# A hybrid decoder step on one core: the inversion's transfers issued side by side from three queues, and weight splits allowed during a norm's sums

## The chip, the cores and the metric

One Trainium2 chip; the kernel runs on one of its cores. The metric is the device time of one execution in microseconds, the median of several runs.

## The reference

One step of a decoder layer over two groups of rows: a prompt of 256 rows and 8 samples of 8 rows, so 320 columns in all when the activations are held transposed (d_model 2048 as 16 chunks of 128 partitions by 320 columns). All tensors are fp32.

```python
mod = silu(c) @ w_ada + b_ada                     # 2048 -> 6*2048
h = rmsnorm(x, g_pre_mix) * (1 + sc1) + sh1
proj = h @ w_in                                   # 2048 -> 5136: q, k, v, z, a, b, u
# group A: conv and silu on q, k, v; 8 heads of 128, chunked gated delta rule
lmat = strict_lower(kb @ k.T * decay)             # per chunk and head
tinv = inverse(I + lmat)                          # triangular solve
u, w = tinv @ (v * beta), tinv @ (kb * exp(gcum))
# group B: S5 state space, gelu, GLU with w_glu, rmsnorm
mix = concat([o, y5]) @ w_out
x = x + gt1 * rmsnorm(mix, g_post_mix)
h = rmsnorm(x, g_pre_ffn) * (1 + sc2) + sh2
f = (silu(h @ w_gate) * (h @ w_up)) @ w_down      # d_ff 5632
x = x + gt2 * rmsnorm(f, g_post_ffn)
```

## The kernel before

**Weights.** Every weight matrix goes through TensorE in blocks of 128 x 1024 numbers (512 KB), each a `Seg`, in one written-out list. A block is loaded by SP (`load`, line 467) into one of 12 buffers. For w_in, w_glu, w_out, w_gate, w_up and w_down it is then split (`do_split`, line 496): ScalarE writes the rounded part `whi`, VectorE the rest `wlo`, and TensorE makes three fast products for each 128 x 128 tile (`mm3`, line 504), with the activations split in the same way. w_ada's blocks aren't split. They are used as they are, four at a time, against 9 columns; the sums of 512 columns are evacuated to a buffer of the same 12 (`adaev`) and transposed (`ada_tail`, line 766).

**Order.** The kernel's order is written out by a planner at build time. It keeps a clock for each engine and for the transfers, and walks the list of blocks. Between any two products of a block it calls `tick`, which advances the background work: generators, each of which yields until the operation that it has next would start soon by these clocks (`fits`, line 168). So each engine gets a fixed order, and the chip's semaphores do the rest. The order of the list around the change: w_in's last slab, w_glu (16 blocks, with 2048 columns of w_ada), w_out's first half (the S5 group's rows; 16 blocks, with 1024 columns of w_ada), w_out's second half (the eight heads' rows, 16 blocks), 1024 columns of w_ada (10240 to 11263), and then the FFN.

**The inversion.** In the background of w_glu and of w_out's first half runs the delta rule of the prompt and that of the samples. `invert` (line 1727) inverts two unit triangular matrices of 128 x 128 for each of the 8 heads. The 16 x 16 diagonal blocks of all of them are turned, through DRAM, into one tile with one block on each partition: 6 writes (the blocks to `inv0`, zeros to `inv1` and `inv2`), 8 small reads into Y, then a substitution in 15 steps on VectorE, 16 small write-backs (from Y and X), 4 reads into Wc and Tc. Products of 32 x 32 and 64 x 64 tiles on TensorE put the blocks together. `chunks` (8 heads, three at a time) then needs the result; `samples` needs none of it and runs beside it. When both are done the heads are ready for w_out's second half.

In the planner a transfer is due to start when its operands are free. What counts for a transfer's output is also the last write to it, by whatever engine, and a DRAM tensor counts as one piece:

```python
for r in (rd.get(k), la.get(k)):
    if r and r[1] != eng:
        t = max(t, r[0] + 0.2)
```

so a transfer that writes `inv1` waits until the one before it is due to have landed.

**The norm ahead of the FFN.** `residual` (line 2373) sums squares over all chunks with products against ones, makes the row factors, and starts `modulate2` (line 2408) for the 16 chunks, four at a time, which writes the FFN's split input h2. From the sums on until four chunks of h2 are written out, `quiet` is set, and `pump` (line 443) splits no further block. `pump` otherwise splits up to 4 blocks ahead (`AHEAD`) of those loaded. `fetch` (line 437) loads the next block whenever more than 3 (`WRES`) of the 12 buffers are free.

Of the kernel before, what the change touches and what calls it, by code (L numbers as in the profile page):

```python
# [23 lines left out]
N = NP + NS  # L24
# [86 lines left out]
class Layer:  # L111
# [36 lines left out]
            e += x * (n - 1)  # L148
        return [(nm, i) for i in range(f // g, e // g + 1)]

    def _start(self, eng, outs, ins, same):

        t = 0.0
        rd, la = self.rd, self.la
        for ap in ins:
            for k in self._keys(ap):
                r = rd.get(k)
                if r:
                    t = max(t, r[0] + (same if r[1] == eng else 0.2))
        for ap in outs:  # L160
            for k in self._keys(ap):
                for r in (rd.get(k), la.get(k)):
                    if r and r[1] != eng:
                        t = max(t, r[0] + 0.2)
                t = max(t, self.war.get(k[0], 0.0) + 0.2)
        return t

    def fits(self, eng, outs, ins):

        c = self.clk  # L170
        t = self._start(eng, outs, ins, 0.0)
        if eng == "PE":
            return t <= c["now"] + self.EPS_PE
        return (eng == "SP" or c[eng] <= c["now"] + self.LIM) and t <= max(c[eng], c["now"]) + self.EPS
# [268 lines left out]
    def pump(self, force=-1):  # L443

        self.fetch()
        while self.ns < min(self.cur + self.AHEAD, self.nl):
            s = self.segs[self.ns]
            if self.ns > force and (self.quiet or s.t > self.clk["now"] or s.split and len(self.wfree) < 3):
                break
            if s.split:  # L450
                self.do_split(s)
                self.wput(s.raw)
            self.ns += 1

    AHEAD, WRES = 4, 3

    def ws(self, name, dt=F32):

        i = self.wfree.pop(0)
        t = self._slot(self.wp.tile([128, 1024], dt, name=name, tag="ws%d" % i, bufs=1), "ws%d" % i, 1)  # L460
        self.wslot[t.name] = i
        return t
# [217 lines left out]
    def xw(self, name="xw"):  # L680
        return self._slot(self.mp.tile([128, 356], F32, name=name, tag="xw", bufs=self.CAP["xw"]), "xw", self.CAP["xw"])

    def dma(self, out, in_, eng=None):
        n = 1
        for d in out.shape:
            n *= d
        q = "SP" if eng in (None, self.nc.sync) else "ACT" if eng is self.nc.scalar else "POOL"
        if self.dry:
            self.sig = q, (out,), (in_,)
            return  # L690
        self.stage_end = max(self.stage_end, self._dma(q, n, out, in_))
        return (eng or self.nc.sync).dma_start(out, in_)
# [1034 lines left out]
    def invert(self):  # L1727

        nc, V, G = self.nc, self.V, self.G
        L = self.L  # L1730
        q_ = nc.sync
        yield from self.take("xw", 7)
        yield from self.take("t4")
        v = lambda t: t[:, :256].rearrange("p (h q) -> p h q", h=8)
# [1 line left out]
        dL, dT, dW = (self.dp.tile([4, 32, 16, 32], F32, name="inv%d" % i) for i in range(3))  # L1736
        Tc = [self.xw("Tc") for _ in range(2)]
        Wc = [self.xw("Wc") for _ in range(2)]
# [7 lines left out]
        yield  # L1746
        flat = lambda d: d.rearrange("b r (c h) q -> c (b r) (h q)", c=2)
        for c in range(2):
            yield from self.p.dma(flat(dL)[c], Tc[c][:, :256], q_)
            for d in (dT, dW):  # L1750
                yield from self.p.dma(flat(d)[c], Wc[0][:, :256], q_)
        G.memset(X[:, 0:256:17], 1.0)
        G.memset(T, 0.0)
        yield
# [1 line left out]
        Yv = Y[:, :256].rearrange("p (r q) -> p r q", r=16)  # L1756
        blk = lambda d, s, b: d[b, 16 * s:16 * s + 16, :, 16 * s:16 * s + 16].rearrange("r h q -> h r q")
        for s in range(2):
            for b in range(4):
                p0 = 64 * s + 16 * b  # L1760
                yield from self.p.dma(Yv[p0:p0 + 16], blk(dL, s, b), q_)
        yield
        yield from self.p.ts(Y[:, :256], Y[:, :256], -1.0, OP.mult)
        for i in range(1, 16):
# [10 lines left out]
        for t, d in ((Yv, dW), (Xv, dT)):  # L1775
            for s in range(2):
                for b in range(4):
                    p0 = 64 * s + 16 * b
                    yield from self.p.dma(blk(d, s, b), t[p0:p0 + 16], q_)
        yield  # L1780
        for t, d in ((Wc, dW), (Tc, dT)):
            for c in range(2):
                yield from self.p.dma(t[c][:, :256], flat(d)[c], q_)
        yield
        Pt = [X, Y]

# [621 lines left out]
    def modulate2(self, kt, rm, rs):  # L2408
        x = self.M[kt]
        yield from self.p.mul(x, x, rm)  # L2410
        yield from self.p.add(x, x, self.xr[kt][:, :N], eng=self.V if kt < self.QUIET else self.G)
        a, sh = self.A[:, kt, :], self.mod[:, 48 + kt, :]
        t = self.xw("h2t")
        yield from self.p.stt(t[:, :NP], x[:, :NP], a[:, 0:1], rs[:, :NP], OP.mult, OP.mult)
        v = t[:, NP:N].rearrange("p (b i) -> p b i", i=8)
        e = self.G
        yield from self.p.mul(t[:, NP:N], x[:, NP:N], rs[:, NP:N], eng=e)
        yield from self.p.mul(v, v, a[:, 1:9, None].to_broadcast([128, 8, 8]), eng=e)
        yield from self.p.add(v, v, sh[:, 1:9, None].to_broadcast([128, 8, 8]), eng=e)
        yield  # L2420
        hl = self.p3.tile([128, 2, N], F32R, name="h2", bufs=16)
        yield from self.p.act(hl[:, 0, :NP], t[:, :NP], AF.Identity, bias=sh[:, 0:1])
        yield from self.p.copy(hl[:, 0, NP:], t[:, NP:N])
        yield
        yield from self.p.stt(hl[:, 1, :NP], t[:, :NP], sh[:, 0:1], hl[:, 0, :NP].bitcast(F32), OP.add, OP.subtract)
        yield from self.p.sub(hl[:, 1, NP:], t[:, NP:N], hl[:, 0, NP:].bitcast(F32))
        self.h2[kt] = hl
# [4 lines left out]
    def ffn(self):  # L2432
        I = self.I

        def start():
            self.bp_close()
            self.p3 = self.p12.enter_context(self.tc.tile_pool(name="p3", bufs=1))
            self.await_(lambda: self.mod_ready.issuperset(range(48, 80)))
            self.set_A(0, 16, 64, "g_pre_ffn")
            self.await_(lambda: "xr" in self.flags)  # L2440
            self.bg(self.residual(), front=True)

        self.fn(start)
        self.items += self.ada_set(self.ADA[4], self.ADA[5])
        self.fT = {}
# [6 lines left out]
        def fbuf():  # L2452
            self.fbase = self.mp.tile([128, 13, 2, N], F32R, name="f", tag="xcat")

        def gu(s, w, f, bank=None):
            self.await_(lambda: hasattr(self, "h2") and all(k in self.h2 for k in range(s.k0, s.k0 + s.nk)))
            if f == 0 and s.k0 == 0 and w == "g":
                fbuf()
            for m in range(s.ncol // 128):
                key = (w, f + m)  # L2460
                if s.k0 == 0:
                    self.gps[key] = self.mbank(bank[m] if bank else self.rot())
                ps = self.gps[key]
                self.mm3(s, ps[:, :N], m, act_h, s.k0 == 0, s.k0 + s.nk == KT)
                if s.k0 + s.nk == KT:
                    ps = self.gps.pop(key)
                    if w == "g":
                        t = self.gs = self.xw("gs")
                        self.act(t[:, :N], ps[:, :N], AF.Silu)
                        self.gsd[f + m] = t  # L2470
                    else:
                        self.bg(self.f_tail(f + m, ps), front=True)
# [3 lines left out]
        for k0 in range(0, KT, 4):  # L2476
            segs.append(Seg(wg, k0, 4, 0, 256, lambda s: gu(s, "g", 0, ("bA", "bA"))))
            segs.append(Seg(wu, k0, 4, 0, 256, lambda s: gu(s, "u", 0, ("bB", "bB"))))
            if k0 % 8:
                segs.append(Seg(wg, k0 - 4, 8, 256, 128, lambda s: gu(s, "g", 2, ("mm",))))  # L2480
                segs.append(Seg(wu, k0 - 4, 8, 256, 128, lambda s: gu(s, "u", 2, ("mm",))))
# [173 lines left out]
```

## Time and profile before

| | us |
|---|---|
| median of 3 runs | 1825.05 |
| lowest, highest | 1821.77, 1828.55 |
| the profiled execution | 1823.18 |
| its span, first to last instruction | 1821.4 |
| mean granted TensorE clock in it | 0.977 of full speed |

The span is what the profile's rows divide up. The granted clock is 1 at 2.4 GHz and 0.5 at 1.2 GHz.

### The profile page before, as it was taken

The page shows a single profiled execution, that of the slowest core. Times are in us where ns is not written, and L with a number is a line of the kernel's source. Part 1 is how long each engine was busy: PE and PEld are TensorE (multiplying, and loading weights), DVE is VectorE, ACT ScalarE, POOL GpSimd, SP SyncE. Part 2 cuts the span into 40 slices and gives each one's busy share as a digit, 9 for nine tenths or more (in the row PEclk, how much of TensorE's full clock was granted, in tenths as well). Part 3 has the DMA queues.
Part 4 walks back from the last instruction along what each step waited for, and adds up shares of the span by engine and source line. Part 5 has one row for each costly group of instructions (what it writes and reads, how often), then busy time and mean ns, then how long its engine had stood idle before and what let it go on. Part 6 is the DMA issues. An engine that isn't in the chain of part 4 may idle for free.

```text
span 1821.4 us, 32727 instructions
## 1 busy us (share of the span) xinstructions
PE 1731.8 (95%) x12961; PEld 1600.4 (88%) x12961; DVE 987.7 (54%) x1840; ACT 768.9 (42%) x1439; POOL 335.0 (18%) x439
## 2 busy tenths in 40 slices
PE   7899998898999889997999999999999999999997
PEld 4678997776787769995999999999999999999997
DVE  3587842788865556677633434444443444444455
ACT  3433334677744434664433333333333333333343
POOL 1000185556132212065300000000000000000043
PEclk8999998999999989998999999999999999999998
DMA  8898744776858956758465565554565545655452
GB/s 275 297 369 287 193 111 129 230 217 209 262 172 257 301 172 179 225 165 289 128 185 174 150 183 169 149 150 122 153 176 151 151 119 152 180 150 149 117 154 80
DMA packets 501262, 340.66 MB, mean 187 GB/s; under 512 B 45355, under 2 KB 452619, under 8 KB 500781
## 3 DMA queue, kind: packets, MB, share of 16 engines
q1 hardware_dynamic: 483904, 332.41, 59.5%
q10 hardware_dynamic: 16838, 5.93, 1.3%
q8 instruction: 102, 1.67, 0.4%
q14 instruction: 50, 0.41, 0.1%
q0 software_dynamic: 368, 0.24, 0.1%
HBM read 323.22 MB, written 14.54 MB: 185 GB/s over the span
## 4 chain that ended last, share of the span: by engine, by line
PE 67%; DVE 3%; ACT 1%; issue 1%; DMA 1%; ACTq 0%; SPq 0%; DVEq 0%
PE ps_mm L319 34%; PE ps_bA L319 17%; PE ps_bB L319 14%; PE ps_ax L319 2%; DVE acc L281 1%; DVE wlo L502 1%; PE ps_bA L333 1%; ACT hT L264 0%; DVE u L281 0%; PE ps_mm L333 0%; DVE P L281 0%; DMA inv<-Y 0%; DMA raw<-in_w_ada_dram 0%; ACT whi L501 0%; DMA S<-in_state_delta_dram 0%
## 5 line engine op out<-in xcount | busy, mean ns | idle before, releaser
L502 DVE TENSOR_TENSOR wlo<-raw,whi 128x1024 fp32r<-128x1024 f32 (+2 forms) x441 | 502.6, 1142 | 554.3 <-ACT whi L501 327.2
L501 ACT ACTIVATE whi<-raw 128x1024 fp32r<-128x1024 f32 (+2 forms) x441 | 424.4, 965 | 412.3 <-DVE wlo L502 309.4
L319 PE MATMUL ps_mm<-h,whi 128*128 128x320 f32 x1376 | 303.4, 308 | 0.0
L319 PE MATMUL ps_mm<-hT,whi 128*128 128x320 f32 x1204 | 290.6, 328 | 2.9 <-ACT hT L264 1.5
L319 PEld LDWEIGHTS ps_mm<-h,whi 128*128 128x128 f32 x1376 | 229.9, 187 | 0.8 <-issue 0.8
L319 PEld LDWEIGHTS ps_mm<-hT,whi 128*128 128x128 f32 x1204 | 202.8, 193 | 14.9 <-issue 6.2
L319 PE MATMUL ps_mm<-h,wlo 128*128 128x320 f32 x688 | 211.6, 307 | 0.0
L319 PE MATMUL ps_mm<-hT,wlo 128*128 128x320 f32 x602 | 189.2, 314 | 2.2 <-DVE wlo L502 2.2
L319 PE MATMUL ps_bA<-h,whi 128*128 128x320 f32 x736 | 166.3, 313 | 3.2 <-DVE h L281 3.0
L319 PE MATMUL ps_bB<-h,whi 128*128 128x320 f32 x704 | 156.0, 309 | 0.0
L319 PE MATMUL ps_mm<-f,whi 128*128 128x320 f32 x704 | 155.5, 308 | 0.0
L281 POOL TENSOR_TENSOR sqa<-acc 128x320 f32<-128x320 f32 x1 | 0.7, 722 | 841.1 <-DVE acc L281 841.1
L319 PEld LDWEIGHTS ps_bA<-h,whi 128*128 128x128 f32 x736 | 125.9, 192 | 4.5 <-DVE h L281 3.3
L319 PEld LDWEIGHTS ps_mm<-h,wlo 128*128 128x128 f32 x688 | 128.9, 187 | 0.0
L319 PEld LDWEIGHTS ps_bB<-h,whi 128*128 128x128 f32 x704 | 118.4, 189 | 0.8 <-issue 0.8
L319 PEld LDWEIGHTS ps_mm<-hT,wlo 128*128 128x128 f32 x602 | 115.5, 192 | 3.5 <-DVE wlo L502 3.5
L319 PEld LDWEIGHTS ps_mm<-f,whi 128*128 128x128 f32 x704 | 117.3, 187 | 0.8 <-ACT whi L501 0.8
L319 PE MATMUL ps_bA<-h,wlo 128*128 128x320 f32 x368 | 115.1, 313 | 1.7 <-DVE wlo L502 1.7
L319 PE MATMUL ps_mm<-f,wlo 128*128 128x320 f32 x352 | 108.5, 308 | 0.4 <-DVE wlo L502 0.4
L319 PE MATMUL ps_bB<-h,wlo 128*128 128x320 f32 x352 | 108.6, 308 | 0.0
L319 PE MATMUL ps_ax<-raw,cs 128*32 128x512 f32 (+2 forms) x832 | 99.6, 588 | 6.9 <-DMA raw<-in_w_ada_dram 6.9
L319 PE MATMUL ps_mm<-hx,whi 128*128 128x320 f32 x328 | 81.1, 333 | 3.3 <-ACT whi L501 3.3
(594 smaller groups left out, 2900.7 us busy)
## 6 DMA issues: line engine op xcount, KB each, us to landing
raw<-in_w_ada_dram SPq DMA_DIRECT2D x180, 512.0 KB
raw<-in_w_gate_dram SPq DMA_DIRECT2D x88, 512.0 KB
raw<-in_w_up_dram SPq DMA_DIRECT2D x88, 512.0 KB
raw<-in_w_in_dram SPq DMA_DIRECT2D x66, 512.0 KB
raw<-in_w_down_dram SPq DMA_DIRECT2D x64, 512.0 KB
raw<-in_w_out_dram SPq DMA_DIRECT2D x32, 512.0 KB
raw<-in_w_down_dram SPq DMA_DIRECT2D x64, 192.0 KB
raw<-in_w_glu_dram SPq DMA_DIRECT2D x16, 512.0 KB
```

The source lines that it names most:

```text
L281: return e.tensor_tensor(out, a, b, op=op)
L319: return self.T.matmul(out, lhsT, rhs, start=start, stop=stop)
L333: return self.T.transpose(out, in_, self.ident[b:b + p, b:b + p])
L501: return (self.S.activation(s.hi[:, :w], s.raw[:, :w], AF.Copy), self.V.tensor_tensor(s.lo[:, :w], s.raw[:, :w], s.hi[:, :w].bitcast(F32), ...
L502: self.V.tensor_tensor(s.lo[:, :w], s.raw[:, :w], s.hi[:, :w].bitcast(F32), op=OP.subtract))
```

## The change

The planner gets a flag `beside`: a transfer that has it no longer counts the transfers that last wrote its output. All transfers of `invert` get it. The 6 writes and the 16 write-backs move from SP's queue to ScalarE's, the 4 last reads to POOL's; the 8 reads into Y stay on SP. While the FFN's start is under way (`deep`, from the start of `residual` to the first product with w_gate), `pump` may go on during `quiet` and beyond 4 blocks, until two blocks that need a split lie ahead. In `modulate2` the residual add of chunks 2 and 3 moves from VectorE to POOL.

```diff
-    def _start(self, eng, outs, ins, same):
+    def _start(self, eng, outs, ins, same, dma=False):
...
-                    if r and r[1] != eng:
+                    if r and r[1] != eng and not (dma and r[1] == "DMA" and r is rd.get(k)):
                         t = max(t, r[0] + 0.2)
...
     def fits(self, eng, outs, ins):
 
         c = self.clk
-        t = self._start(eng, outs, ins, 0.0)
+        dma = eng[-1] == "*"
+        eng = eng.rstrip("*")
+        t = self._start(eng, outs, ins, 0.0, dma)
...
     def pump(self, force=-1):
 
         self.fetch()
-        while self.ns < min(self.cur + self.AHEAD, self.nl):
+        while self.ns < self.nl:
             s = self.segs[self.ns]
-            if self.ns > force and (self.quiet or s.t > self.clk["now"] or s.split and len(self.wfree) < 3):
+            if sum(x.split for x in self.segs[self.cur:self.ns]) > 1 if self.deep else self.ns >= self.cur + self.AHEAD:
+                break
+            if self.ns > force and (self.quiet and not self.deep or s.t > self.clk["now"] or s.split and len(self.wfree) < 3):
                 break
...
-    def dma(self, out, in_, eng=None):
+    def dma(self, out, in_, eng=None, beside=False):
...
-            self.sig = q, (out,), (in_,)
+            self.sig = q + "*" * beside, (out,), (in_,)
...
-        q_ = nc.sync
+        q_, qs, ql = nc.sync, nc.scalar, nc.gpsimd
...
         for c in range(2):
-            yield from self.p.dma(flat(dL)[c], Tc[c][:, :256], q_)
+            yield from self.p.dma(flat(dL)[c], Tc[c][:, :256], qs, beside=True)
             for d in (dT, dW):
-                yield from self.p.dma(flat(d)[c], Wc[0][:, :256], q_)
+                yield from self.p.dma(flat(d)[c], Wc[0][:, :256], qs, beside=True)
...
-                yield from self.p.dma(Yv[p0:p0 + 16], blk(dL, s, b), q_)
+                yield from self.p.dma(Yv[p0:p0 + 16], blk(dL, s, b), q_, beside=True)
...
-                    yield from self.p.dma(blk(d, s, b), t[p0:p0 + 16], q_)
+                    yield from self.p.dma(blk(d, s, b), t[p0:p0 + 16], qs, beside=True)
         yield
         for t, d in ((Wc, dW), (Tc, dT)):
             for c in range(2):
-                yield from self.p.dma(t[c][:, :256], flat(d)[c], q_)
+                yield from self.p.dma(t[c][:, :256], flat(d)[c], ql, beside=True)
...
-        yield from self.p.add(x, x, self.xr[kt][:, :N], eng=self.V if kt < self.QUIET else self.G)
+        yield from self.p.add(x, x, self.xr[kt][:, :N], eng=self.V if kt < 2 else self.G)
...
             self.bg(self.residual(), front=True)
+            self.deep = True
...
             if f == 0 and s.k0 == 0 and w == "g":
+                self.deep = False
                 fbuf()
```

## Rows read from the trace of the kernel before

**Rows 1.** The page: TensorE and the others, busy time, share of the span, instructions.

```profile
PE 1731.8 (95%) x12961; PEld 1600.4 (88%) x12961; DVE 987.7 (54%) x1840; ACT 768.9 (42%) x1439; POOL 335.0 (18%) x439
```

**Rows 2.** Busy time by stretch: length, PE, PEld, DVE, ACT, POOL; clock, DMA share, GB/s.

```profile
555.00:648.00 93.00, 86.47 (x627) 69.27 (x625) 52.68 (x131) 42.60 (x76) 24.88 (x42) 1.00 0.91 288
648.00:683.00 35.00, 26.62 (x742) 22.92 (x742) 17.58 (x41) 10.04 (x21) 3.45 (x8) 0.85 0.50 159
683.00:769.00 86.00, 85.47 (x658) 77.60 (x656) 56.81 (x147) 51.09 (x150) 10.66 (x20) 1.00 0.64 191
769.00:827.00 58.00, 57.38 (x391) 56.49 (x393) 45.79 (x62) 32.56 (x58) 37.05 (x41) 1.00 0.65 200
827.00:876.00 49.00, 35.74 (x208) 26.28 (x205) 37.46 (x71) 19.51 (x40) 28.35 (x52) 0.79 0.67 234
876.00:1821.40 945.40, 935.32 (x6381) 927.87 (x6379) 407.43 (x479) 338.64 (x443) 47.06 (x63) 0.99 0.52 151
```

**Rows 3.** Timeline of SP's queue: start, duration of the issue, transfer, count.

```profile
556.14 0.34 SPq L692 DMA_DIRECT2D inv<-Tc  x1
...
559.51 0.33 SPq L692 DMA_DIRECT2D Y<-inv  x1
...
579.19 1.86 SPq L692 DMA_DIRECT2D Y<-inv  x1
...
601.10 0.33 SPq L692 DMA_DIRECT2D inv<-Y  x1
...
642.93 1.15 SPq L692 DMA_DIRECT2D Wc<-inv  x2
```

**Rows 4.** Timeline of PE: start, duration, product, count, [idle before it <- releaser].

```profile
648.21 1.29 PE L319 MATMUL ps_bA<-Wc,L 32*32 32x32 f32 x128
...
659.91 0.21 PE L319 MATMUL ps_bB<-Tc,X 32*32 32x32 f32 x1 [3.32 <-issue]
...
666.20 0.21 PE L319 MATMUL ps_bB<-Tc,Y 32*32 32x32 f32 x1 [4.69 <-issue]
...
769.14 0.45 PE L319 MATMUL ps_mm<-hz,whi 128*128 128x320 f32 x2
```

**Rows 5.** The tile inv: its write-backs on SP, shortest/median/longest issue in ns.

```profile
L692 SPq DMA_DIRECT2D inv<-Y x8: 327/644/1988, 601.1 to 626.8; - x8
L692 SPq DMA_DIRECT2D inv<-X x8: 423/559/1892, 627.7 to 642.1; - x8
```

**Rows 6.** Transfers of POOL's queue: KB each, us from issue to landing.

```profile
vr<-in_b_ada_dram POOLq DMA_DIRECT2D x1, 48.0 KB, 5.4
wr<-in_w_conv_dram POOLq DMA_DIRECT2D x1, 48.0 KB, 8.6
```

**Rows 7.** Timeline of ScalarE: one issue of a transfer, and one split.

```profile
70.30 0.44 ACTq L692 DMA_DIRECT2D craw<-in_c_re_dram  x1
...
592.09 1.06 ACT L501 ACTIVATE whi<-raw 128x1024 fp32r<-128x1024 f32 x1 [5.62 <-DVE P L281]
```

**Rows 8.** Timeline of PE where the FFN starts.

```profile
847.58 1.11 PE L333 MATMUL ps_mm<-ident,adaev 128*128 128x128 f32 x4 [8.37 <-ACT adaev L264]
...
850.93 0.63 PE L319 MATMUL ps_bA<-h,wlo 128*128 128x320 f32 x1 [1.71 <-DVE wlo L502]
...
867.03 0.63 PE L319 MATMUL ps_bA<-h,whi 128*128 128x320 f32 x1 [3.03 <-DVE h L281]
```

**Rows 9.** Timelines of VectorE, ScalarE and POOL in the norm ahead of the FFN.

```profile
835.18 0.49 DVE L281 TENSOR_TENSOR ms<-ps_bA,rs 128x320 f32<-128x320 f32 x1 [4.69 <-PE ps_bA L319]
...
838.05 0.49 DVE L281 TENSOR_TENSOR u<-u,xr 128x320 f32<-128x320 f32 x1
...
845.76 0.86 POOL L281 TENSOR_TENSOR u<-u,xr 128x320 f32<-128x320 f32 x1
...
846.00 1.04 ACT L501 ACTIVATE whi<-raw 128x1024 fp32r<-128x1024 f32 x1
...
849.65 1.23 DVE L502 TENSOR_TENSOR wlo<-raw,whi 128x1024 fp32r<-128x1024 f32 x1
```

More of the change, by code (lines that the diff above doesn't have):

```diff
@@ L455 @@
     AHEAD, WRES = 4, 3
+    deep = False
     def ws(self, name, dt=F32):
```

## The prediction

> **What bounds the kernel now.** I read the engines' busy times first: TensorE is busy 1731.8 us of the span [rows 1], so only TensorE's holes can be won. Then the busy time by stage [rows 2]: the reader subtracts TensorE's busy time from each stretch. From 876 us on it lacks 10.1 of 945.4 us, and nothing in the change reaches that part. From 683 to 827 us it lacks 1.1. What is left is 555 to 648 us (6.5 idle; the inversion's transfers run here), 648 to 683 us (8.4 idle and a granted clock of 0.85, 35 × 0.15 = 5.3 more; the inversion's matmuls) and 827 to 876 us (13.3 idle, clock 0.79; the norm ahead of the FFN). About 40 us is all that the change can touch. The timelines of SP, PE, ScalarE and VectorE in these stretches gave the rest.
>
> **Part 1, the chain of the inversion.** The order on SP [rows 3] shows it: first write 556.14, reads of Y from 559.51 to 579.19, write-backs from 601.10, last reads 642.93, while the first matmul on the result starts at 648.21 [rows 4]. 92 us, of which VectorE's substitution takes about 15 (the last read is issued by 581.05, lands within the 5.3 us below, near 586, and the write-backs begin at 601). The write-backs alone spread over 41.8 us, because the planner held each one until the one before it was due to have landed. The new flag takes that wait away. Worked out: the 8 reads cost SP about 0.53 each, 4.2 us, and land within the 5.3 us that the last reads took (642.93 to 648.21); Y is there near 569 and not near 586. The 16 write-backs go out in 16 × 0.6 (the medians of both kinds [rows 5]), 9.6 us, and land in 5.3: 15 in place of 41.8. The last 4 reads move to POOL's queue, where a transfer takes 5.4 to 8.6 us to land [rows 6], against 5.3. The chain ends 17 + 27 − 2, about 42 us earlier.
>
> What this buys: the chain has to end before w_out's second half, which needs the eight heads. That half starts at 769.14 [rows 4], and in the 86 us before it TensorE lacks 0.5 us [rows 2]. So TensorE does not wait for the heads. It takes their matmuls in between the blocks of w_out's first half; earlier heads only push these blocks back. What is late next is TensorE's own list. Value: 0. Bounds: 0, and the gaps that the chain itself makes. Of these there are two, 3.32 and 4.69 us within the 32x32 matmuls [rows 4], released by nothing the profile shows, with the clock's dip after them (0.85 over the stretch): 8.4 + 5.3 = 13.7 us. The same matmuls are issued afterwards, into a stretch with more transfers under way (DMA share 0.91 against 0.50), so I keep the gaps. The other small holes of 555 to 648 us, 6.5 us, may shrink: the inversion holds 7 of the 12 xw buffers and a sample needs 3, so earlier release lets two samples and the chunks overlap. I take −2, bounds 0 to −6.5.
>
> **Part 1, the cost on ScalarE.** 6 writes and 16 write-backs are now ScalarE instructions. One issue there took 0.44 us [rows 7]; on SP the write-backs took 0.33 to 1.99 [rows 5]. The 6 cost 6 × 0.44 = 2.6 us and fall beside ScalarE's idle time. The 16 come as one block (the planner books 0.1 us each, 1.6 together) and hold ScalarE for 9.6 us, 5.3 at the least and 16 if each took 1.0. Queued behind them are the `whi` halves of the next w_glu blocks, the tanh of the gates and the copy of `adaev`; TensorE waits for each of these in its own order. The cover is ScalarE's idle time in this stretch, for instance 5.62 us before 592.09 [rows 7]. If it is used up the cost is 9.6 − 5.6 = 4.0 us of TensorE; I take +4, bounds 0 and +9.6. Each issue also waits for its source (Tc, Wc's zeros, X, Y), but the planner asks for that before it emits, so the waits are short.
>
> **Part 1, POOL.** The 4 last reads wait on POOL for the 16 write-backs. Queued behind them are a sample's two masks and the squares of the GLU's rows, and TensorE waits for the masks. The result lands 0.1 to 3.3 us later than through SP, and now TensorE's first 32x32 matmul may stand at the head of its queue meanwhile, where today it starts without a wait. I take +1.5, bounds 0 and +3.3. SP loses 26 of its issues, but no wait of TensorE for a weight load is among the holes from 555 to 683 us, so that is worth 0.
>
> **Part 2, the two FFN blocks.** Today the first block of w_gate gets its `whi` at 846.00 and its `wlo` at 849.65, after the norm, and TensorE waits 1.71 us for it at 850.93, having waited 8.37 for the evacuation of the w_ada columns that stands behind that `whi` on ScalarE, and 3.03 for h2 later [rows 8, 9]. VectorE is idle for 4.69 us during the sums [rows 9], so there is room for a split. But the block is not there to be split. A block is loaded only when more than 3 of the 12 weight buffers are free. While `quiet` holds, the eight blocks of w_ada's columns 10752 to 11263 hold 8 of them, the evacuated sums of columns 10240 to 10751 hold 1 (`ada_tail` gives it back only after `quiet`, and until then the eight cannot be used up), and 3 are kept: 12. So `pump` stops at the last loaded block, whatever `deep` allows, and the first w_gate block is loaded and split where it is now, after `quiet`. Only the w_up block can come somewhat earlier, and TensorE does not wait for that one today. The two residual adds go from VectorE (0.49 each) to POOL (0.86) [rows 9]: VectorE gains 1.0 us, POOL's row of work for the first four h2 tiles grows by 1.7, with about 1 us of slack. Value of part 2: 0. Bounds: +2 (POOL late by 0.7 to 2) and −9 (below).
>
> **Sum.** The profiled execution took 1823.18 us, 1.8 around its span. 0 − 2 + 4 + 1.5 + 0 = +3.5 gives 1826.7. The runs' median is 1825.05, 1.9 above that execution, so I say 1828: the same within what a measurement of this kernel can tell (0.5%, 9 us).
>
> **Rivals.**
> A. *Faster: the inversion's gaps close.* If the 32x32 matmuls, at their new place, come with wide matmuls in between, both gaps and the dip go: 3.5 − 13.7 = −10.2, 1815. For it: the first 128 of them took 1.29 us without a gap [rows 4]. Against: the next 256 had two. It decides from about 9 us of the 13.7. The Trainium skill ("Runtime: NRT & Kernel Launch", Instruction fetch mechanics) says that refilling an engine's instruction memory is mostly hidden; if the gaps are such refills, the trace disagrees today, and by that rule they would go.
> B. *Slower: the block of issues stops TensorE.* If none of ScalarE's idle time covers it, TensorE loses 9.6 us where I booked 4 and then a spell at 1.2 GHz, as after the gaps at 659.91 and 666.20, 5.3 us: 3.5 + 5.6 + 5.3 = +14, 1839. For it: ScalarE's results are waited for in TensorE's order. Against: 5.62 us of idle time on ScalarE. It decides from an issue of 0.8 us on.
> C. *The FFN blocks are split during the sums after all.* Then the `whi` leaves the copy's way (1.04 us), the 1.71 goes and up to 3.03, and some of the dip (clock 0.79 over 49 us): −5.8 − 3, with part 1 as above: −5.3, 1820; alone it is worth −9. For it: the idle 4.69 us. Against: the count of buffers.
> D. *POOL's reads come late.* If each of the 4 reads waited its turn for a landing of 8.6 us in place of 5.3, the chain ends 13 us later than booked, and TensorE stands for a part of it, 4 us: 1832. The Trainium skill ("SBUF — State Buffer", SBUF: two separate sides) says that descriptors of POOL's transfers are written by GpSimd and are kept from it while VectorE runs some of its copies, and that ScalarE's or SP's queue avoids this; no run here shows it yet. By the rule the landing is longer than the rows' 8.6.
>
> **How the numbers follow.** The forecast (1820 to 1834) 0.48, A 0.13, B 0.18, C 0.11, D 0.10. Faster by over 0.5%, below 1815.9: most of A and half of C, 0.18. Slower, above 1834.2: most of B, a little of D and of the forecast, 0.23. The same: 0.59. The range goes from A's far side, 1813, to B, 1841.
>
> **What would show it.** Right: SP shows no write-back any more, ScalarE a block of 16 issues of some 0.6 us each; the first 32x32 matmul comes about 40 us earlier; w_out's second half starts within 6 us of 769; the first w_gate block still has its `wlo` after the first h2 tiles. Wrong: a `whi` of w_gate between the sums and 838 us (C); no "issue" gap among the 32x32 matmuls (A); a TensorE wait of over 5 us on ScalarE beside the block of issues, or on POOL's landing (B, D). The forecast also falls if the new order of the list moves TensorE's holes elsewhere, after 683 us, where there are none now.

## The result, and the profile after

| | before | after |
|---|---|---|
| median, us | 1826.38 (4 runs) | 1837.29 (4 runs) |
| lowest, highest | 1821.77, 1828.55 | 1836.00, 1840.38 |
| span of the profiled execution | 1821.4 | 1838.6 |

The ratio is 1.0075 (95% interval 1.0052 to 1.0098): slower, by 11 us in the medians. That is inside the range, outside the forecast's own 1820 to 1834, and within 2 us of rival B's 1839. The profile's first part of the kernel after, to be held against [rows 1], shows TensorE busy 6.7 us longer; the rest of the longer span is idle time.

```profile
PE 1738.5 (95%) x12961; PEld 1603.3 (87%) x12961; DVE 987.6 (54%) x1838; ACT 770.7 (42%) x1441; POOL 340.9 (19%) x445
```

**Cut at the same instructions.** The stage borders of [rows 2] fall on other work now, so I cut both traces at three TensorE instructions that bear the same work: the samples' first `sP,kb` product, the first `hz` product (w_out's second half), and the transposes of `adaev` ahead of the FFN (at 847.58 before). Ahead of the first mark TensorE's order did not change, yet its time varies from 554.6 to 563.8 us over the executions profiled here (e5 aside). Whoever compares spans takes this scatter along. The windows, of before and then of after; the first number behind each is its length:

```profile
558.40:769.14 210.74, 196.19 (x1993) 168.08 (x1993) 124.06 (x309) 102.15 (x242) 36.63 (x64) 0.98 0.74 230
769.14:847.58 78.44, 69.45 (x473) 61.62 (x471) 60.08 (x91) 41.02 (x76) 46.17 (x58) 0.96 0.76 248
847.58:1821.40 973.82, 958.86 (x6500) 948.89 (x6500) 430.46 (x519) 349.70 (x465) 66.28 (x98) 0.99 0.51 150
```

```profile
562.72:786.32 223.60, 203.33 (x1992) 172.38 (x1993) 122.77 (x308) 102.64 (x243) 37.92 (x68) 0.95 0.73 224
786.32:869.94 83.62, 69.93 (x473) 61.64 (x471) 64.78 (x95) 42.04 (x78) 48.84 (x64) 0.95 0.64 202
869.94:1838.60 968.66, 956.89 (x6500) 947.25 (x6500) 427.92 (x513) 349.85 (x465) 69.21 (x94) 0.99 0.52 151
```

The counts of matmuls agree to within one, so each stretch holds the same products. The first is 12.9 us longer: idle 20.3 against 14.6 us (+5.7), busy 203.3 against 196.2 (+7.1 for the same products; the clock, below, accounts for it). The second is 5.2 longer, the third 5.2 shorter. The sum is +12.9.

**The first stretch.** ScalarE's timeline after, where the write-backs now stand:

```profile
588.62 0.58 ACT L266 ACTIVATE adaev<-ps_ax 128x512 f32<-128x512 f32 x1
588.64 0.84 ACTq L697 DMA_DIRECT2D inv<-Y  x2
589.10 0.43 ACT L266 ACTIVATE gt<-ps_mm 128x320 f32<-128x320 f32 x1
589.58 5.44 ACTq L697 DMA_DIRECT2D inv<-Y  x6
595.05 5.79 ACTq L697 DMA_DIRECT2D inv<-X  x8
600.94 0.38 ACT L266 ACTIVATE sP<-ps_bA 128x256 f32<-128x256 f32 x1 [11.41 <-DMA raw<-in_w_ada_dram]
```

From 588.64 to 600.84, 12.2 us, ScalarE issues 16 transfers, and it computes nothing from 589.53 on. A row of the timeline joins issues that follow one another and holds the time between them too, so 0.76 us for each is the pace of the block and not the length of an issue. The issues themselves, shortest/median/longest in ns:

```profile
L697 ACTq DMA_DIRECT2D inv<-Y x8: 310/432/525, 588.6 to 594.6; - x8
L697 ACTq DMA_DIRECT2D inv<-X x8: 309/459/642, 595.1 to 600.4; - x8
```

Together they take 6.9 us, the 0.44 of [rows 7] for each. The other 5.3 us lie between them, and 4.7 of those in three waits: 2.66 us up to 593.70, 0.73 up to 597.93 and 1.29 up to 599.53. By the trace's record of semaphores (the counters by which instructions wait for one another) each of the three issues waits for the counter of an earlier write-back of the block, and starts 0.02 us after that one has landed. In this program the transfers of SP and ScalarE share eight such counters, and POOL's have eight of their own, so a long row of transfers has to wait for its own landings.

Behind the block stands `sP`, the evacuation that the next sample's products need. VectorE waits for it, and TensorE for VectorE (VectorE's timeline, then TensorE's; what the dots stand for is left out here and below):

```profile
601.36 0.60 DVE L301 TENSOR_SCALAR kr<-ps_bA,dk 64x128 f32<-64x128 f32 x2 [9.68 <-ACT sP L266]
...
602.11 1.19 PE L321 MATMUL ps_bA<-sP,kb 128*128 128x128 f32 x4 [7.99 <-DVE kr L301]
```

The releaser named for TensorE is VectorE's `kr`; that one had itself waited 9.68 us for ScalarE. One has to follow the chain a step back to find the block. Then the inversion's small products, TensorE's timeline:

```profile
611.65 1.29 PE L321 MATMUL ps_bA<-Wc,L 32*32 32x32 f32 x128
...
619.14 0.21 PE L321 MATMUL ps_bA<-Tc,X 32*32 32x32 f32 x1 [4.00 <-issue]
...
630.90 0.69 PE L321 MATMUL ps_bA<-L 32*32 32x32 f32 x30 [1.84 <-DVE L L283]
```

and the clock, in windows laid around every spell in which 1.2 GHz was granted in this stretch (the third number from the right is the granted clock), of after and then of before:

```profile
598.80:605.60 6.80, 3.49 (x14) 3.52 (x15) 1.37 (x4) 0.66 (x2) 0.75 (x2) 0.50 0.72 186
619.20:622.60 3.40, 3.40 (x33) 2.98 (x34) 0.79 (x4) 0.00 (x0) 1.22 (x2) 0.50 0.03 8
632.90:646.50 13.60, 13.31 (x192) 9.05 (x177) 4.31 (x10) 6.91 (x15) 2.69 (x8) 0.50 0.47 145
```

```profile
661.10:671.30 10.20, 5.51 (x69) 4.89 (x58) 4.54 (x13) 0.39 (x1) 0.00 (x0) 0.50 0.38 111
```

The first 32x32 product comes 48.9 us behind the first mark, where it was 89.8: 40.9 earlier, as forecast. TensorE is at 1.2 GHz in and behind the 7.99 us hole, behind the gap of 4.00, and for 13.6 us from 632.9 on, behind the run of small products with its last hole of 1.84. At half the clock, half of the busy time is its price: 10.1 us here (1.7 behind the block, 1.7 and 6.7 behind the small products) against 2.8 before, all at the gaps of [rows 4]. The difference of 7.3 is the +7.1 of busy time.

**The second and third stretch.** TensorE's holes and ScalarE's timeline at the FFN's start, which answer to [rows 8, 9]:

```profile
823.55 0.53 PE L321 MATMUL ps_mm<-hz,whi 128*128 128x320 f32 x2 [1.20 <-DVE M L283]
835.54 0.53 PE L321 MATMUL ps_mm<-hz,whi 128*128 128x320 f32 x2 [1.19 <-DVE M L283]
869.94 1.12 PE L335 MATMUL ps_mm<-ident,adaev 128*128 128x128 f32 x4 [10.87 <-ACT adaev L266]
906.04 0.64 PE L321 MATMUL ps_bA<-h,whi 128*128 128x320 f32 x1 [1.66 <-DVE h L283]
```

```profile
868.36 1.04 ACT L506 ACTIVATE whi<-raw 128x1024 fp32r<-128x1024 f32 x1
869.31 0.58 ACT L266 ACTIVATE adaev<-ps_ax 128x512 f32<-128x512 f32 x1
```

The first w_gate block's `whi` still stands behind the sums, ahead of `adaev`: the block is not split in `quiet`. The waits of 1.71 and 3.03 us [rows 8] are gone, and one of 1.66 for `h` has come, 36 us into the third stretch. The wait for `adaev` is 10.87 for 8.37, and two new ones of 1.2 end on VectorE's sums `M`.

### The profile page after: what moved, and what is told of

Read it like the earlier page. It is cut to its first block, busy times and chain, and to the rows that moved or that the text cites. A ratio compares the mean times of both kernels' runs of the same rounds, so it can differ in the third digit from the quotient of the medians.

```text
span 1838.6 us, 32720 instructions
## 1 busy us (share of the span) xinstructions
PE 1738.5 (95%) x12961; PEld 1603.3 (87%) x12961; DVE 987.6 (54%) x1838; ACT 770.7 (42%) x1441; POOL 340.9 (19%) x445
## 4 chain that ended last, share of the span: by engine, by line
PE 75%; DVE 8%; DMA 6%; POOL 5%; ACT 4%; issue 2%; ACTq 0%; SPq 0%; DVEq 0%; POOLq 0%
PE ps_mm L321 37%; PE ps_bA L321 19%; PE ps_bB L321 15%; PE ps_ax L321 3%; POOL bx L283 2%; DVE wlo L507 2%; ACT whi L506 1%; DVE ca L308 1%; DMA raw<-in_w_ada_dram 1%; POOL AB L283 1%; DMA ts<-ts 1%; POOL ctab L283 1%; PE ps_bB L335 1%; DVE acc L283 1%; DMA x<-in_x_prompt_dram 1%
## 5 line engine op out<-in xcount | busy, mean ns | idle before, releaser
L321 PE MATMUL ps_mm<-hx,whi 128*128 128x320 f32 x328 | 81.3, 334 | 3.3 <-ACT whi L506 3.3
```

The lines of the kernel that those rows point to most:

```text
L321: return self.T.matmul(out, lhsT, rhs, start=start, stop=stop)
```

## The experiments

**Theory S**: the block of transfers on ScalarE is the price. **Rival O**: the price is the new order, in which the inversion's small products stand close together. **Rival N**: the second part costs in the norm. Each kernel was timed in 5 rounds beside the kernel before; "stretches" are the three above, in us, against 210.7, 78.4 and 973.8 before; they come from one execution of each kernel.

| kernel | median us | ratio (95% interval) | stretches |
|---|---|---|---|
| after | 1837.29 | 1.0075 (1.0052 to 1.0098) | 223.6, 83.6, 968.7 |
| e1, inversion's part alone | 1841.36 | 1.0087 (1.0066 to 1.0109) | 225.5, 81.2, 973.7 |
| e2, FFN's part alone | 1822.08 | 0.9986 (0.9973 to 0.9999) | 212.4, 81.3, 966.8 |
| e3, write-backs on SP | 1835.08 | 1.0055 (1.0037 to 1.0072) | 220.5, 83.7, 967.2 |
| e5, planner's price 0.76 | 1854.39 | 1.0161 (1.0136 to 1.0186) | (order changed earlier) |
| e6, before and the block | 1838.27 | 1.0081 (1.0059 to 1.0103) | 225.9, 78.4, 974.1 |
| e7, matmuls 30 us later | 1841.42 | 1.0092 (1.0071 to 1.0113) | 225.5, 83.6, 967.2 |
| e8, write-backs on POOL | 1820.47 | 0.9981 (0.9967 to 0.9995) | 209.4, 83.6, 967.7 |
| e9, on three queues | 1832.50 | 1.0040 (1.0023 to 1.0058) | 219.3, 83.6, 967.0 |
| e10, e8 without the FFN's part | 1820.56 | 0.9985 (0.9971 to 1.0000) | 205.0, 80.9, 973.6 |
| e11, e8 with deep alone | 1821.86 | 0.9989 (0.9976 to 1.0001) | 208.5, 80.9, 973.0 |
| e12, e8, first writes on SP | 1822.58 | 1.0000 (0.9986 to 1.0014) | 208.4, 83.7, 967.2 |
| e13, e8 with kt < 2 alone | 1819.32 | 0.9970 (0.9955 to 0.9984) | 207.8, 83.6, 967.6 |

**e1 and e2, one part each.**

```diff
-            self.deep = True                                   # e1, and its reset in gu
-        ... eng=self.V if kt < 2 else self.G)
+        ... eng=self.V if kt < self.QUIET else self.G)
```

> The inversion's part alone: the flag deep and the bound kt < 2 are taken back. Theory S (the block of 16 issues on ScalarE, 588.6 to 600.8 us in the trace after, holds up the evacuation that TensorE's 7.99 us wait at 602.11 ends on, and a spell of low clock follows): the loss sits ahead of 700 us and is there in full, and what the second part gave back at the FFN's start (TensorE's waits of 1.71 and 3.03 us of before are absent after, one of 8.37 became 10.87) is gone, so 1838 to 1843, with the hole of about 8 us near 602. Rival N (the loss comes from the second part, in the norm): the time falls back to 1826.

In e2 the transfers go back: `q_ = qs = ql = nc.sync`, without `beside`.

> The FFN's part alone: the inversion's transfers go through SP, without the new flag, in the order of before; deep and kt < 2 stay. TensorE's order is then that of before. Theory S: no loss, and the waits of 1.71 and 3.03 us at the FFN's start go or shrink: 1821 to 1826. Rival N (the norm's stretch costs): 1830 or more, with a longer wait for the w_ada evacuation ahead of the first FFN matmul. My prediction's own step (the second part is worth 0): 1826.

The loss is the first part's: 1841.36 alone, with a hole of 7.21 us at 593.97. The second part gains a little by itself, 2.6 us by its ratio, whose interval ends just below 1. N falls, and so does my 0 for the second part.

**e3, the write-backs on SP.**

```diff
-yield from self.p.dma(blk(d, s, b), t[p0:p0 + 16], qs, beside=True)
+yield from self.p.dma(blk(d, s, b), t[p0:p0 + 16], q_, beside=True)
```

> As after, but the 16 write-backs go through SP's queue, still beside each other; the first 6 writes stay on ScalarE and the last 4 reads on POOL. Theory S: ScalarE is free between 588 and 601, TensorE's hole of 7.99 us and the 1.8 us of low clock behind it go: 1825 to 1829. Rival O (what costs is the new order: the inversion's matmuls stand in one run where few wide matmuls cover them, whichever queue carries the transfers): the hole shrinks but the time stays at 1833 to 1839.

Theory S, as put, is wrong: 1835.08. A block bites on SP too, as SP's timeline and then ScalarE's and TensorE's show:

```profile
590.78 5.79 SPq L697 DMA_DIRECT2D inv<-Y  x8
596.67 4.76 SPq L697 DMA_DIRECT2D inv<-X  x8
601.48 1.01 SPq L697 DMA_DIRECT2D S<-in_state_delta_dram  x2
602.59 0.45 SPq L477 DMA_DIRECT2D raw<-in_w_glu_dram  x1
```

```profile
608.90 1.06 ACT L506 ACTIVATE whi<-raw 128x1024 fp32r<-128x1024 f32 x1 [8.14 <-DMA raw<-in_w_glu_dram]
...
610.01 0.56 PE L321 MATMUL ps_mm<-hT,whi 128*128 128x320 f32 x2 [1.88 <-ACT whi L506]
```

The 16 transfers hold back SP's next loads by 10.7 us, so ScalarE waits 8.14 for its weight block and TensorE 1.88. That is smaller than 7.99, but the first stretch is still 9.8 longer than before: 3.9 idle, 5.9 of busy time for the same products.

**e5, the planner told the price.** `0.1 if q == "ACT"` becomes `0.76 if q == "ACT"` in `_dma`.

> As after, with one number changed: the planner books 0.76 us for an issue on ScalarE (12.2 us over 16 issues in the trace after) instead of 0.1, and so puts other work of ScalarE between them, in runs of 10 and 6 write-backs. Theory S: the longest stretch that ScalarE is held falls to about 7.6 us, TensorE's wait behind it to 3 or 4 us: 1831 to 1834. Rival O: the order of the inversion's matmuls is what costs, and the time stays at 1835 to 1839.

1854.39, which neither theory expected. The number holds for every transfer that ScalarE issues, so TensorE's order differs from 86 us on, long before the inversion. The run tells nothing of the block.

**e6, the block alone.** The kernel before, with 16 extra writes that nothing reads (the line that makes their two buffers is left out):

```diff
+        for t, d in ((Yv, dY), (Xv, dX)):
+            for s in range(2):
+                for b in range(4):
+                    p0 = 64 * s + 16 * b
+                    nc.scalar.dma_start(blk(d, s, b), t[p0:p0 + 16])
```

> The kernel before, unchanged but for 16 more writes: just ahead of its own write-backs through SP, the same X and Y are also written through ScalarE, 16 issues in one block, to two buffers in memory that nothing reads. The planner is not told of them, so the orders of TensorE, VectorE, POOL and SP are those of before, and the chain of the inversion is as slow as before. Theory S (the block itself is the price: 16 issues of 0.76 us that ScalarE's next results wait behind): TensorE gets a hole of 6 to 10 us that ends on ScalarE or on what it feeds, and a spell of low clock behind it: 1832 to 1836. Rival O (the price is the new place of the inversion's matmuls, and a block alone is covered by ScalarE's idle time): 1825 to 1829.

The orders of TensorE, VectorE, POOL and SP are those of before, instruction for instruction. It costs 13.4 us in the medians. ScalarE's timeline, then TensorE's:

```profile
605.53 6.55 ACTq L1779 DMA_DIRECT2D inv<-Y  x8
612.14 8.24 ACTq L1779 DMA_DIRECT2D inv<-X  x8
620.49 0.31 ACT L264 ACTIVATE sP<-kr 64x128 f32<-64x128 f32 x1 [19.42 <-DMA inv<-X]
...
623.20 0.69 PE L319 MATMUL ps_bA<-ident,kr 128*128 128x64 f32 x2 [11.31 <-ACT kr L264]
```

The block takes 14.9 us, and TensorE gets a hole of 11.31. The 16 issues sum to 7.2 us (medians 0.44 and 0.45); the rest is again waits for earlier transfers to land. The other two stretches stay within 0.4. A block on ScalarE has its price with the order left alone.

**e7, the small products put back.** `self.later(30.0)` and a `yield` ahead of the first 32x32 product.

> As after, with one pause: once the last four reads are issued the inversion sleeps for 30 us of the planner's time, so its 32x32 matmuls come back to about where they stood in the kernel before. The block of 16 issues on ScalarE stays. Theory S: the hole of 8 us near 602 stays, and the time with it: 1834 to 1839. Rival O: the low clock behind the inversion's matmuls (634 to 646 us in the trace after, half speed) goes back to what it was before, and the time falls to 1828 to 1832 although the block is still there.

The hole stays (8.00), the first 32x32 product comes 81.6 us behind the mark, and the time does not fall: 1841.42. The half-speed spell behind the small products is 10.2 us again, as before, with one of 3.4 later, and the busy time falls by 1.4; but 3.3 of idle come on top. Putting the products back does not give the loss back.

**e8 and e9, other queues for the write-backs.** The same line as in e3, with `ql` (POOL), and with `(qs, q_, ql)[(4 * s + b) % 3]`.

> As after, but the 16 write-backs go through POOL's queue, ahead of the four last reads there. Theory S: the hole behind ScalarE goes, and comes back only where POOL's masks for the next sample stand behind the block: with POOL idle for 18 us there in the trace after, 1826 to 1830. Rival O: as with the write-backs on SP (1835.1), 1833 to 1838, since the place of the inversion's matmuls is the same.

> As after, but the 16 write-backs are dealt out over the queues of ScalarE (6), SP (6) and POOL (4), so that no engine is held by more than about 5 us. Theory S: no engine is held long enough to stop TensorE: 1825 to 1829. Rival O: 1833 to 1838.

e8 is the first with the inversion's part that is not slower than before: 1820.47, below both forecasts. TensorE's order moves with it, from 620 us of after on, so e8 alone does not say which of S and O went. POOL's timeline of e8:

```profile
582.59 4.12 POOL L697 DMA_DIRECT2D inv<-Y  x7 [2.48 <-DVE Y L276]
587.00 0.56 POOL L697 DMA_DIRECT2D inv<-Y  x1 [0.29 <-issue]
590.00 0.72 POOL L283 TENSOR_TENSOR gt<-u 128x320 f32<-128x320 f32 x1 [2.43 <-DVE u L308]
590.80 0.88 POOL L283 TENSOR_TENSOR sqa<-sqa,gt 128x320 f32<-128x320 f32 x1
591.62 3.93 POOL L697 DMA_DIRECT2D inv<-X  x7
599.54 0.72 POOL L283 TENSOR_TENSOR gt<-u 128x320 f32<-128x320 f32 x1 [4.00 <-DVE u L308]
```

That is 0.59 us per issue over the first seven, with hardly a wait between them, and POOL still waits for VectorE beside them. The largest holes of the first stretch are now 2.67, 1.90 and 1.62 us. e9 has the orders of TensorE and VectorE of after, unchanged; only the block is dealt out. The wait at the same product falls from 7.99 to 2.13, the first stretch's idle time from 20.3 to 14.8, and the median by 4.8 us (the ratios differ by 6). Part of the block is still there. ScalarE's timeline, in which the last three of its issues take 4.98 us because one of them waits 3.67 for a landing:

```profile
589.22 4.98 ACTq L697 DMA_DIRECT2D inv<-X  x3
594.31 0.38 ACT L266 ACTIVATE sP<-ps_bA 128x256 f32<-128x256 f32 x1 [4.92 <-DMA inv<-X]
```

What stays beside it is clock:

```profile
624.00:641.10 17.10, 16.90 (x241) 11.99 (x241) 6.27 (x17) 8.44 (x18) 4.65 (x12) 0.50 0.46 131
```

So S and O each hold of a part of after. Some 5 us come back when the block is dealt out. The first stretch of e9 is still 8.6 longer than before, 8.4 of it busy time, with 17.1 us at half speed behind the small products. The length of that spell goes with TensorE's order: 13.6 to 17.1 us in the three kernels with after's order (after, e1, e9), 10.2 in the three with before's (before, e2, e6), 3.4 to 6.8 in the four with e8's (e8, e10, e11, e13). That the order causes it is not shown, since no run has after's order with no block at all.

**e10, e11 and e13, the second part taken apart on e8.** TensorE's and SP's orders are the same in all four. e10 has neither line, e11 `deep` alone, e13 `kt < 2` alone.

> The kernel of the run with the write-backs on POOL (1820.5), without the second part: deep and kt < 2 are taken back; the orders of TensorE and SP stay. Theory S: the inversion's part costs nothing once ScalarE is free of the block, 1822 to 1827, and the waits of about 1.7 and 3.0 us come back behind the first FFN matmul. Rival: moving the write-backs to POOL is itself a gain and the second part is worth nothing on top: 1818 to 1822.

> The same, with deep and without kt < 2 (the first four residual sums stay on VectorE). If the second part's gain comes from deep (four whi in a row ahead of the h2 tiles, so no wait of 1.7 or 3.0 us after the first FFN matmul) and its loss of about 2.5 us ahead of that matmul from the two sums moved to POOL: 1817 to 1820, with a wait for the w_ada evacuation of about 8 us in place of 10.7. If the gain comes from kt < 2: 1822 to 1827.

> The fourth of the square: write-backs on POOL, kt < 2 without deep. In the run with deep alone the waits of 1.71 and 3.04 us behind the first FFN matmul are both still there, so the second part's effect should sit in kt < 2: the two waits are gone, the wait for the w_ada evacuation is 10 to 11 us in place of 7.2 to 7.9, and from the first matmul of w_out's second half to the end it takes 1050 to 1052 us (1054.5 with neither, 1053.9 with deep alone, 1051.3 with both): 1819 to 1822. If both lines are needed together: 1053 to 1055 us for that stretch.

From w_out's second half to the end it takes 1054.5 us with neither, 1053.9 with `deep`, 1051.2 with `kt < 2`, 1051.3 with both. In e11 the waits of 1.71 and 3.04 us are there, in e13 they are not. The gain is that of the two sums on POOL, about 3 us in one execution of each: from e10 to e13 the last stretch loses 3.3 us of waits and 2.7 of busy time, and a longer wait for `adaev` takes 2.7 back. `deep` is worth nothing that shows. The medians do not tell it: 1819.32 to 1821.86 with intervals that overlap, and e10 fell in the range of the rival, to which the second part is worth nothing. One reason is scatter: between 750 and 757 us TensorE waits 1.9 to 2.9 us for a sum `M` in e8, e11 and e13, with half speed behind it, and not in e10, though the order up to there is the same.

**e12, no issue on ScalarE at all.** The first six writes go through `q_` too.

> The run with the write-backs on POOL, and the first 6 writes on SP too, so that ScalarE issues nothing for the inversion. Theory S: those 6 took 2.8 us of ScalarE beside its idle time and no wait of TensorE ended on them, so 1818 to 1823, as with them. If a block of 6 on ScalarE has a price too: 1814 to 1817.

1822.58: the six had no price that shows. TensorE's order moved here too, from 10 us behind the first mark on, so a small price could hide in it.

## Why the prediction was right and wrong, point by point

The range held, and the forecast's own line did not: it had +3.5 us, and 11 were measured. Of the signs named beforehand, those for the block on ScalarE, for the 40 us and for the late `wlo` came true; but w_out's second half started at 786.32, not within 6 us of 769, and TensorE waited 7.99 us behind the block.

- **Part 1, the cost on ScalarE (+4).** This step failed. Its price of an issue was right: 0.43 and 0.46 in the medians, 6.9 us for the 16, within the 9.6 booked. What it put at nothing were the waits between issues. It thought of waits for sources alone ("so the waits are short"); of the 5.3 us between the issues, 4.7 were waits for the block's own earlier transfers to land. The cover came out right by luck. I took 5.6 us of ScalarE's idle time; what covered the block was TensorE's own work, which lasted until 594.1, 5.5 us after the block's start. The block took 12.2 us, the evacuation and VectorE behind it 1.3 more: 12.2 - 5.5 + 1.3 = 8.0, the hole. The clock behind it adds 1.7. So 9.7 in place of 4 by the trace; dealing the block out (e9) gives 5 to 6 back and leaves 3.8 of it (2.13 and 1.7 of clock); on before's own order (e6) it is 13.4. I had also named what stands behind the block wrongly in part: not `whi`, tanh or `adaev`, but a sample's evacuation, which the planner had put there because it books 0.1 us per issue.
- **What the earlier chain buys (0, gaps kept).** This step failed too. The chain did end 41 us earlier and TensorE did not need it. But the new order was not free: the gaps of 3.32 and 4.69 us became one of 4.00 and a wait of 1.84 for VectorE, and yet the clock behind the small products takes 8.4 us where it took 2.8; two waits of 1.2 on `M` lengthen the second stretch by 2.8 (e1). I had counted the order's change as neutral. Of rival A the gaps shrank, but not by its mechanism: 41 other products stand among the 32x32 ones, where it was 85. (The dip's 5.3 us in the prediction counts idle time at the low clock too; over the busy time it is 2.8.)
- **POOL (+1.5).** Too high: the four reads landed in 3.5 and 2.9 us (median of each pair), not 5.4 to 8.6, and no wait of TensorE ends on them. So rival D falls for this kernel, though in e9 the same reads took 7.1 and 6.4, and in e5 TensorE waited 3.56 us for one pair. In e8 POOL's 16 KB writes landed in 4.6 and 4.4 us while VectorE was splitting weights. The Trainium skill ("SBUF — State Buffer", SBUF: two separate sides) has some of VectorE's copies starve such transfers; the splits are `TENSOR_TENSOR` instructions and not copies, so no run here shows it.
- **Part 2 (0).** The first w_gate block was not split during the sums, so rival C fell; the count of buffers was the argument, and no trace shows the count itself. What I passed over is the other line: two sums on POOL free VectorE in its busiest stretch. I had priced it at 1.0 us gained and 1.7 lost; e10 against e13 shows 3.3 us gained.
- **Small holes of 555 to 648 us (-2).** After doesn't show a gain from them, and no run isolates them. With the write-backs on POOL the first stretch is 205.0 to 209.4, 1 to 6 us under before, which can come from the chain and the holes together; the scatter is as large.

Rival B had the right place, the block on ScalarE with a hole and a spell at 1.2 GHz, and I gave it 0.18 because the block seemed covered. That its 1839 came within 2 us is luck. It wanted issues of 0.8 us and no cover; the issues took 0.43 to 0.46, 5.5 us were covered, and 5.6 of the first stretch's 12.9 us are the clock behind the small products, which it does not have. What stays open is why the half-speed spell behind the small products is 13.6 to 17.1 us long in after's order and 3.4 to 6.8 in e8's. The number of other products among the 32x32 ones in TensorE's order does not settle it: 41 in after and e9, 66 in e3 (1835.1 us) and 67 in e12 (1822.6), 85 before, 120 in e8.

## What to carry to other kernels

A transfer that a computing engine issues costs that engine's time, and a block of them costs what stands behind it: look for the first result that another engine waits for there, and count from the moment when that engine runs dry. Look between the issues as well: a joined row of the timeline hides waits, and here they were almost half of the block. An order that a planner writes is only as good as its prices: booked at 0.1 us, a block of 12.2 us looks free, and at 1.0 (POOL's price) the same planner spreads it. When an edit moves an order, compare traces at marks that bear the same work, and take one run that keeps the order and adds only the suspect (e6), and one that keeps the new order and removes it (e9).

## What the runs showed of the hardware that was not expected

The block on ScalarE was long by waits, not by issues. The same 16 KB write (64-byte runs) was issued in 0.43 to 0.46 us on ScalarE (medians of after and e6) and in 0.56 on POOL (e8); on SP the medians were 0.45 to 0.64 [rows 5] (e3), with single issues of up to 1.99. ScalarE's blocks lasted 12.2 and 14.9 us all the same, because issues waited for earlier transfers to land, 2.66 us at the longest in after and 3.53 in e6. POOL's first seven issues in e8 took 4.12 us, with hardly a wait. The first six writes, of 128 KB each, took 0.33 to 0.46 us apiece on ScalarE but for one of 1.56 (after): eight times the bytes did not make an issue longer.
